# Spreading the output weights' eleven sums and moving later copies and the query weights' DMAs to ScalarE's queue, in one decoder layer

## Chip, cores and metric

The kernel runs on one core of one Trainium2 chip. The metric is the device time of one execution in microseconds (us). TensorE (PE) multiplies matrices, VectorE (DVE) and ScalarE (ACT) work element by element, GpSimd (POOL) does masks and issues the DMAs that add, SyncE (SP) issues nearly all other DMAs.

## The reference, cut to what matters

One layer of a decoder trunk in fp32: 512 positions of width 1024, and 256 memory tokens.

```python
h = rms_norm(x, norm_mix)
q, k, v, u, gate_b, gate_c, g_a, g_b = split(h @ w_in)
o_a = stick_breaking_attention(q, k, v)              # 8 heads x 64, causal
y_b = gate_b * causal_depthwise_conv(gate_c * u, conv_w)
merged = sigmoid(g_a) * (o_a @ w_branch_a) + sigmoid(g_b) * (y_b @ w_branch_b)
x = x + merged @ w_mix_out
x = x + memory_cross_attention(rms_norm(x), rms_norm(mem), w_mem_q, w_mem_kv, w_mem_o)
gate, up = split(rms_norm(x) @ w_ffn_in)              # hidden width 2816
x = x + (silu(gate) * up) @ w_ffn_out
return rms_norm(x, norm_final)
```

## The kernel before

Every fp32 product is made of three matmuls on parts: a tile is split into a high part (ACT's cast, line 156 and its like) and a low part (DVE's subtraction, line 157), and `mm3` multiplies high by high, high by low and low by high. A weight tile of 512 KB is loaded by SP (`load_w`, line 148, tile `wr`), cast by ACT (`wh`) and subtracted by DVE (`wl`); each of the three has a ring of four buffers.

Three of the products use a scheme of seven products of half-size blocks instead of eight (query projection of the memory attention, both FFN products). Its weight forms are sums of weight blocks, made on the way:

- **Output weights.** `w_ffn_out` comes as eleven tiles of four quarters each (`wfo_d[j]`). For each of them a DRAM tile `sums[j]` is formed by DMAs alone. `out_sums(j)` returns four steps: two plain copies from DRAM to DRAM (768 KB and 256 KB, line 569, issued on SP), then an adding DMA of two quarters of the weights (512 KB, line 572, issued on POOL), and twice an adding DMA of one quarter of the sums onto another (256 KB, line 572). Each step waits for the transfers of the step before it. The sums are read back only in the last product, from 709.9 us on.
- **Query weights.** `w_mem_q` comes as four tiles (heads) of 1 MB. For each head `form_load` loads the tile into SBUF (tile `pq`, two buffers, line 642), `form_sums` makes four additions on DVE (line 648) and `form_store` writes the tile to DRAM (`qsums`, line 652). `pair_forms` reads it back in the memory attention (line 810).

The order around the change is written by hand. A counter `started` advances by one at each call of `tick`. `job(at, steps, lag)` puts the steps of one sum on ticks `at`, `at + lag`, and so on; `tick` issues what stands on its number. Ticks 0 to 16 stand in the loop over the sixteen steps of the stick-breaking attention (four pairs of heads by four key blocks) and its end, 17 to 24 in the branch loop over eight output tiles, 25 to 28 in the mix-out product at every second tile, 29 and 30 in the memory keys' loop, 31 after the first half of the memory values, 32 to 35 in the four heads of the memory attention. `SUMS_AT` holds the tick of the first step of each of the eleven sums; the first `SPARSE` of them have a lag of 2 ticks, the others of 1. `after(i, last)` orders an instruction behind another in the schedule without a wait on the chip: a DMA that waits for no data is issued as soon as its queue comes to it.

In the attention stage SP also carries the query and key moves (line 361): for each pair of heads, parts of a tile are copied between the two halves of the partitions, six moves for the queries and three for the keys, some of which wait for earlier ones to land. POOL carries the causal masks (line 417) and, in tick 9's iteration, the store of the memory factors `rmd` (line 557).

In the memory keys' loop the row of squares' means goes to DRAM and back (`turned_row`, lines 226 and 228, on SP), since it has to be turned from a row to a column.

The branch loop's calls on the query weights:

```python
loaded_at, stored_at = {0: 0, 2: 1, 4: 2, 5: 3}, {3: 0, 5: 1, 7: 2}
summed_at = {2: 0, 4: 1, 6: 2, 7: 3}
```

The last store comes after the mix-out product's second tile.

Of the kernel before, what the change touches and what calls it, by code (L numbers as in the profile page):

```python
# [34 lines left out]
FIRST = 4  # L35
LIGHT = 3
BEHIND = 6
SUMS_AT = (0, 2, 4, 20, 22, 24, 25, 26, 27, 28, 30)
SPARSE = 3

O_Q, O_K, O_V, O_U, O_GB, O_GC, O_A, O_B = 0, 512, 1024, 1536, 2048, 2560, 3072, 4096

# [2 lines left out]
def hybrid_layer(ctx: ExitStack, tc: tile.TileContext, xT_d, memT_d, mem_d, cols_d, wv_d, win_d,  # L45
                 wbr_d, wmix_d, wmq_d, wmk_d, wmv_d, wmo_d, wfi_d, wfo_d, gfin_d, out):
    nc = tc.nc
# [16 lines left out]
    def nm(s):  # L64
        count[0] += 1
        return f"{s}{count[0]}"
# [4 lines left out]
    def tmp(s, cols=512):  # L71
        return tpool.tile([P, cols], F32, tag="t", name=nm(s), padded_shape=[P, 512])
# [34 lines left out]
    def after(i, earlier):  # L107
        for e in earlier:
            tc.add_manual_dep(i.ins, e.ins.name, mybir.DependencyInfo(
                mybir.DependencyClass.NoSync, mybir.DependencyReason.DATA), reason="order")  # L110
# [33 lines left out]
    def load_w(src, cols=P):  # L144

        k = D // cols
        raw = wpool.tile([P, D], F32, tag="wr", name=nm("wr"))
        i = nc.sync.dma_start(raw, src)
        loads.append(i)
        if count[1] < FIRST:  # L150
            count[1] += 1
            chained(i)
        hi = wpool.tile([P, k, cols], F32R, tag="wh", name=nm("wh"))
        lo = wpool.tile([P, k, cols], F32R, tag="wl", name=nm("wl"))
        h2, l2 = (t.rearrange("p k c -> p (k c)") for t in (hi, lo))
        after(nc.scalar.copy(h2, raw), lead[-1:])  # L156
        lows.append(nc.vector.tensor_tensor(out=l2, in0=raw, in1=f(h2), op=ALU.subtract))  # L157
        return hi, lo
# [292 lines left out]
    def scores(p, kt):  # L451
        c0, n = span(kt)
        keys = slice(kt * P, (kt + 1) * P)
        zs[p, kt] = []
        for hs in heads_of(kt):
            bank = ztile("z")
            zs[p, kt].append(bank)
            for i, h in enumerate(hs):
                for part in range(2):
                    nc.tensor.matmul(bank[:, i * n:(i + 1) * n], ks[p][h][:, keys],  # L460
                                     qs[p][h][part][:, c0:], start=i + part == 0, stop=part == 1,
                                     skip_group_check=True)
        for hs, bank in zip(heads_of(kt), zs[p, kt]):
            w = len(hs) * n
            z = bank[:, :w]
            e = tmp("e")[:, :w]
            nc.scalar.activation(e, z, AF.Abs)
            nc.scalar.activation(e, e, AF.Exp, scale=-1.0)
            nc.scalar.activation(e, e, AF.Ln, bias=1.0)
            nc.vector.scalar_tensor_tensor(out=e, in0=z, scalar=0.0, in1=e, op0=ALU.max,  # L470
                                           op1=ALU.add)
            causal(by_head(e, n))
            urgent.append(lambda *last, e=e, hs=hs: fails(p, kt, hs, e, n, last))
# [86 lines left out]
    def quarters(w):  # L560
        return w.rearrange("p (s c) -> p s c", s=4)

    def in_dram(tag):
        return dpool.tile([P, 4, 512], F32, tag=tag, name=nm(tag))

    sums = [in_dram(f"sums{j}") for j in range(NJ)]

    def copied(to, of):
        return lambda *last: after(nc.sync.dma_start(to, of), last)

    def added(to, of):
        return lambda *last: after(nc.gpsimd.dma_start(to, of, accum_op=ALU.add), last)  # L572

    def out_sums(j):
        t, w = sums[j], quarters(wfo_d[j])
        return ([copied(t[:, 1:4, :], w[:, 1:4, :]), copied(t[:, 0:1, :], w[:, 3:4, :])],
                [added(t[:, 0:4:3, :], w[:, 0:2, :])], [added(t[:, 1:2, :], t[:, 0:1, :])],
                [added(t[:, 2:3, :], t[:, 1:2, :])])

# [2 lines left out]
    def job(at, steps, lag=1):  # L582
        for n, some in enumerate(steps):
            jobs.setdefault(at + n * lag, []).extend(some)
# [19 lines left out]
    settle_behind()  # L604
    qsums = [in_dram(f"qsums{h}") for h in range(MH)]
    for j, n in enumerate(SUMS_AT):
        job(n, out_sums(j), 2 if j < SPARSE else 1)

    for i in range(len(steps) + 1):
        tick(*exps[-1:])  # L610
# [10 lines left out]
        if i + 1 < len(steps):  # L621
            to = lambda: scores(*steps[i + 1])
# [15 lines left out]
    mg, mgs, qraws = [], [], {}  # L638

    def form_load(h, last):  # L640
        qraws[h] = prepool.tile([P, 4, 512], F32, tag="pq", name=nm("pq"))
        after(nc.sync.dma_start(qraws[h], quarters(wmq_d[h])), last)

    def form_sums(h, last, *steps):

# [3 lines left out]
                                          op=ALU.add), last)  # L649

    def form_store(h):
        nc.sync.dma_start(qsums[h], qraws.pop(h))

    def mem_split(k2, last):
        mk = xpool.tile([P, 2, MEM], F32, tag="x", name=nm("mk"))
# [15 lines left out]
    for m in range(KD):  # L671
        sig = []
        for j in range(2):
            if (m, j) not in gates:
                gate(m, j)
            t = gates.pop((m, j))
            sigmoid = nc.scalar.activation(t, t, AF.Sigmoid)
            after(sigmoid, exps[-2:])
            sig.append(t)
        if m in summed_at:  # L680
            form_sums(summed_at[m], [sigmoid], (0, 0, 3), (3, 1, 3))
        w = load_w(wbr_d[m])
        for j in (1, 0):
            if m == 0 and j == 0:
                gate(EARLY, 0)
            ps = mmtile("br")
            gemm(ps, w, (oT, yb)[j], 4 * j)
            nc.vector.tensor_tensor(out=sig[j], in0=ps, in1=sig[j], op=ALU.mult)
        nc.vector.tensor_tensor(out=sig[0], in0=sig[0], in1=sig[1], op=ALU.add)
        merged.append(split(sig[0], "m"))  # L690
        if m in stored_at:
            form_store(stored_at[m])
        if m in loaded_at:
            form_load(loaded_at[m], [sigmoid])
        if m in summed_at:
            form_sums(summed_at[m], [sigmoid], (1, 1, 0), (2, 2, 1))
        tick(sigmoid)
        sigmoids.append([sigmoid])
        if m < KD // 2:
            mem_split(m, [sigmoid])  # L700
# [56 lines left out]
    def residual(w_dram, act, old, gain, formed):  # L757
# [4 lines left out]
        for m in range(KD):  # L762
            w = load_w(w_dram[m])
            ps = mmtile("r")
            gemm(ps, w, act)
            if old is None:
                xm = xpool.tile([P, S], F32, tag="x", name=nm("x"))
                after(nc.sync.dma_start(xm, xT_d[m * P:(m + 1) * P, :]), sigmoids[m // 2 - 4])
            else:
                xm = old[m]  # L770
            nc.vector.tensor_tensor(out=xm, in0=ps, in1=xm, op=ALU.add)
            xs.append(xm)
            if old is None and m % 2:
                tick(lows[-1])
                if qraws:
                    form_store(MH - 1)
            raw = f(unit("xr"))
            nc.scalar.activation(raw, xm, AF.Copy, scale=gain[:, m:m + 1])
            if m % 2:
                xf.append(formed(even, raw))  # L780
            else:
                even = raw
            if m == 0:
                nc.scalar.activation(acc, xm, AF.Square)
            else:
                sq = tmp("sq")
                nc.scalar.activation(sq, xm, AF.Square)
                nc.vector.tensor_tensor(out=acc, in0=acc, in1=sq, op=ALU.add)
# [87 lines left out]
    for m in range(KD):  # L876
        w = load_w(wmk_d[m])
# [8 lines left out]
        t = tmp("km", MEM)  # L886
# [52 lines left out]
    for h in range(MH):  # L939
        q = qgot[h]  # L940
        scs = []
        for t2 in range(2):
            ps = ztile("sc")
            scs.append(ps)
            for i in range(2):
                t = 2 * t2 + i
# [5 lines left out]
        for t2 in range(2):  # L952
# [14 lines left out]
            for i in range(2):  # L967
                t = 2 * t2 + i
# [25 lines left out]
        for j in range(2):  # L994
# [3 lines left out]
            for m in range(MT):  # L998
                w = vm[m][c // 512]
# [245 lines left out]
    def one_cast(j):  # L1245
        if j % 2 == 0:
            n = min(2, NJ - j)
            raw = ows["q3"] = wpool.tile([P, 2, 512], F32, tag="wr", name=nm("wr"))
            nc.sync.dma_start(raw[:, :n, :], wfo_d[j:j + n, :, 0:512].rearrange("j p c -> p j c"))
        raw = ows["q3"][:, j % 2, :]  # L1250
        pool, tag = (fpool, "wg") if j in (BEHIND, BEHIND + 2) else (wpool, ("wh", "wl")[j % 2])
        w = pool.tile([P, 2, 512], F32R, tag=tag, name=nm("wq"))
        nc.scalar.copy(w[:, 0, :], raw)
        ows[5, j] = w[:, 0, :], w[:, 1, :]
        return raw, *ows[5, j]
# [75 lines left out]
    n = uses.index((NF - 2, 5))  # L1331
# [23 lines left out]
    with tc.manual_schedule(engines={mybir.EngineType.PE, mybir.EngineType.Activation,  # L1355
# [58 lines left out]
        for j in range(2, NJ - 2):  # L1414
# [6 lines left out]
            if NJ - 2 - LIGHT <= j + 1 < NJ - 2 + 1:  # L1421
                n = j + 1 - (NJ - 2 - LIGHT)
                if n < LIGHT:
                    t34_of(n, halves(acts[n][1])[0])
        last = NJ - 2, NJ - 1
# [93 lines left out]
        w = one_cast(NJ - 1)  # L1519
# [184 lines left out]
```

## Time and profile before

| | |
|---|---|
| median of 3 runs | 835.94 us (835.62 to 836.13) |
| profiled execution | 837.15 us, span 835.4 us |
| mean granted TensorE clock | 0.998 |
| TensorE busy | 826.5 us, 99% of the span, 4518 matmuls |
| VectorE busy | 689.6 us, 83% |
| ScalarE busy | 481.8 us, 58% |
| GpSimd busy | 105.9 us, 13% |
| DMA on SP's and ACT's own queues | 130.96 MB and 0.28 MB |
| DMA on POOL's queue | 23.21 MB |
| first copy to last copy of the sums on SP | 27.8 to 373.7 us |
| query weights: first load to last store on SP | 186.7 to 300.4 us |

Idle time is put down to the instruction that ended it. "SPq" and "ACTq" are the queues' own instructions: a DMA's duration there is the time of its issue, and its landing is given apart. A transfer's issue holds the instructions behind it on the same engine.

### The profile page before, as it was taken

Reading aid. Unit: us, or ns where it says so; the run is one execution under the profiler, and the core shown is the slowest. Engines: PE = TensorE matmul, PEld = TensorE weight load, DVE = VectorE, ACT = ScalarE, POOL = GpSimd, SP = SyncE. Lnnn points to the kernel's source line nnn. Section 1 sums busy time; section 2 is a strip of 40 time slices with the busy share of each in tenths; the row PEclk is TensorE's granted clock in tenths of the full one; section 3 lists DMA queues with packets and bytes.
Section 4 is the critical chain, followed back from the end, with each engine's and each line's share of the span. In section 5 each row is a group of like instructions: output and inputs, shape, how many; then the busy total and the mean of one; then the engine's idle time right before and its main releaser. Section 6 shows DMA issues by size and latency. Waiting matters only on the chain.

```text
span 835.4 us, 12382 instructions
## 1 busy us (share of the span) xinstructions
PE 826.5 (99%) x4518; PEld 718.7 (86%) x4518; DVE 689.6 (83%) x1146; ACT 481.8 (58%) x836; POOL 105.9 (13%) x131
## 2 busy tenths in 40 slices
PE   9999999999999999999999999999999999999996
PEld 7888888888888888888999789999999999888885
DVE  7879899995665557865677689999999999999886
ACT  7567777674332345645665556645555555576664
POOL 0022331120010011210000131111111110000301
PEclk9999999999999999999999999999999999999999
DMA  8667965224588999898445626677777773565552
GB/s 303 202 189 179 222 141 121 82 81 171 216 225 291 253 312 294 194 218 279 125 136 189 167 50 170 165 179 189 207 179 196 181 181 97 166 217 198 178 187 100
DMA packets 58926, 155.24 MB, mean 186 GB/s; under 512 B 6545, under 2 KB 7825, under 8 KB 57842
## 3 DMA queue, kind: packets, MB, share of 16 engines
q1 hardware_dynamic: 46226, 130.96, 46.6%
q0 software_dynamic: 12352, 23.21, 18.5%
q8 instruction: 35, 0.57, 0.3%
q10 hardware_dynamic: 288, 0.28, 0.1%
q14 instruction: 25, 0.20, 0.1%
HBM read 144.08 MB, written 29.37 MB: 208 GB/s over the span
## 4 chain that ended last, share of the span: by engine, by line
PE 95%; DMA 2%; DVE 1%; ACT 1%; issue 0%; DVEq 0%; SPq 0%; ACTq 0%
PE z L1078 13%; PE p L1389 12%; PE pr L161 8%; PE pr L162 8%; PE pr L163 8%; PE y L1073 5%; PE r L161 3%; PE r L163 3%; PE r L162 3%; PE v L288 3%; PE y L1081 2%; PE v L1073 2%; PE qz L834 2%; PE br L162 2%; PE br L161 2%; PE br L163 2%
## 5 line engine op out<-in xcount | busy, mean ns | idle before, releaser
L156 ACT CAST wh<-wr 128x1024 fp32r<-128x1024 f32 x76 | 79.7, 1051 | 113.0 <-issue 45.1
L161 PE MATMUL pr<-xgh,wh 128*128 128x512 f32 x288 | 112.7, 391 | 0.0
L162 PE MATMUL pr<-xgl,wh 128*128 128x512 f32 x288 | 112.4, 390 | 0.0
L163 PE MATMUL pr<-xgh,wl 128*128 128x512 f32 x288 | 112.3, 390 | 0.0
L157 DVE TENSOR_TENSOR wl<-wr,wh 128x1024 fp32r<-128x1024 f32 x76 | 93.6, 1232 | 9.8 <-ACT wh L156 9.5
L163 PEld LDWEIGHTS pr<-xgh,wl 128*128 128x128 f32 x288 | 54.1, 188 | 11.5
L161 PEld LDWEIGHTS pr<-xgh,wh 128*128 128x128 f32 x288 | 54.1, 188 | 10.6
L162 PEld LDWEIGHTS pr<-xgl,wh 128*128 128x128 f32 x288 | 54.1, 188 | 10.5
L1026 POOL DMA_DIRECT2D ws<-in_w_ffn_in_dram x22 | 26.6, 1207 | 237.5 <-PE pt L987 57.1
L1078 PE MATMUL z<-xd,wf 128*128 128x256 f32 x360 | 47.5, 282 | 0.0
L1110 ACT COPY sa<-z 128x256 f32<-128x256 f32 x44 | 16.5, 374 | 52.1 <-PE z L1078 52.0
L1078 PEld LDWEIGHTS z<-xd,wf 128*128 128x128 f32 x360 | 44.9, 190 | 0.1
L1170 DVE TENSOR_TENSOR wf<-wg,wf 128x1024 fp32r<-128x1024 f32 (+1 forms) x44 | 43.1, 979 | 1.5
L1170 DVE TENSOR_TENSOR wl<-wr,wh 128x1024 fp32r<-128x1024 f32 x33 | 41.1, 1247 | 3.6 <-ACT wh L1237 3.6
L368 DVE TENSOR_TENSOR g<-pr,r0b 128x512 f32<-128x512 f32 x16 | 11.0, 689 | 34.2 <-PE pr L163 34.2
L1237 ACT CAST wh<-wr 128x1024 fp32r<-128x1024 f32 x33 | 34.5, 1049 | 6.9 <-PE xt L1474 2.5
L1078 PE MATMUL z<-xf,wf 128*128 128x256 f32 x264 | 35.4, 283 | 0.0
L1078 PE MATMUL z<-xc,wf 128*128 128x256 f32 x264 | 35.1, 282 | 0.0
L1078 PEld LDWEIGHTS z<-xf,wf 128*128 128x128 f32 x264 | 33.4, 192 | 0.1
L1078 PEld LDWEIGHTS z<-xc,wf 128*128 128x128 f32 x264 | 33.0, 190 | 0.0
L572 POOL DMA_DIRECT2D sums<-sums x22 | 18.5, 851 | 94.7 <-DMA sums<-in_w_ffn_out_dram 47.4
L572 POOL DMA_DIRECT2D sums<-in_w_ffn_out_dram x11 | 15.7, 1469 | 98.7 <-DMA sums<-in_w_ffn_out_dram 98.2
(377 smaller groups left out, 2313.8 us busy)
## 6 DMA issues: line engine op xcount, KB each, us to landing
wr<-in_w_in_dram SPq DMA_DIRECT2D x36, 512.0 KB, 4.1
ws<-in_w_ffn_in_dram SPq DMA_DIRECT2D x22, 512.0 KB, 4.6
wg<-in_w_ffn_in_dram SPq DMA_DIRECT2D x22, 512.0 KB, 4.5
ws<-in_w_ffn_in_dram POOLq DMA_DIRECT2D x22, 512.0 KB, 5.8
wr<-sums SPq DMA_DIRECT2D x22, 512.0 KB, 4.4
sums<-in_w_ffn_out_dram SPq DMA_DIRECT2D x11, 768.0 KB, 8.1
wr<-in_w_ffn_out_dram SPq DMA_DIRECT2D x16, 512.0 KB, 4.5
sums<-in_w_ffn_out_dram POOLq DMA_DIRECT2D x11, 512.0 KB, 10.2
```

The costliest lines, as they stand in the source:

```text
L156: after(nc.scalar.copy(h2, raw), lead[-1:])
L157: lows.append(nc.vector.tensor_tensor(out=l2, in0=raw, in1=f(h2), op=ALU.subtract))
L161: nc.tensor.matmul(ps, a[0], b[0], start=start, stop=False, **kw)
L162: nc.tensor.matmul(ps, a[0], b[1], start=False, stop=False, **kw)
L163: nc.tensor.matmul(ps, a[1], b[0], start=False, stop=stop, **kw)
L572: return lambda *last: after(nc.gpsimd.dma_start(to, of, accum_op=ALU.add), last)
L1026: nc.gpsimd.dma_start(s13, a[:, 0:4:3, :], accum_op=ALU.add)
L1073: nc.tensor.matmul(ps, hi, both[0], start=i < 3 and k == 0, stop=False, skip_group_check=True)
L1078: nc.tensor.matmul(ps[:, :HS], a, b, start=i < 3 and k == 0 and j == 0, stop=k == KP - 1 and j == 2, skip_group_check=True)
L1170: nc.vector.tensor_tensor(out=lo, in0=src, in1=f(hi), op=ALU.subtract)
L1237: nc.scalar.copy(hi, raw)
L1389: nc.tensor.matmul(res[i][s2], a[:, ts], b, start=j == 0 and n == 0, stop=n == 2 and j == (BEHIND - 1 if (i, s2) == (5, 1) else NJ - 1))
```

## The change

`SUMS_AT` becomes wider: sum 0 stays at tick 0; sums 1, 2 and 3 start at ticks 3, 6 and 9 (2, 4 and 20 before); sums 4, 5 and 6 at 20, 22 and 24 (22, 24 and 25 before); sums 7 to 10 at 26, 28, 30 and 32 (26, 27, 28 and 30 before). The first four sums, not three, have a lag of 2. The copies of sums 4 to 10 are issued by ACT instead of SP; those of sums 0 to 3 stay on SP. The query weights' four loads and four stores are issued by ACT instead of SP. All adding DMAs stay on POOL. No arithmetic, tile or transfer is added or left out.

```diff
-SUMS_AT = (0, 2, 4, 20, 22, 24, 25, 26, 27, 28, 30)
-SPARSE = 3
+SUMS_AT = (0, 3, 6, 9, 20, 22, 24, 26, 28, 30, 32)
+SPARSE = 4
...
-    def copied(to, of):
-        return lambda *last: after(nc.sync.dma_start(to, of), last)
+    def copied(queue, to, of):
+        return lambda *last: after(queue.dma_start(to, of), last)
...
-    def out_sums(j):
+    def out_sums(j, queue):
         t, w = sums[j], quarters(wfo_d[j])
-        return ([copied(t[:, 1:4, :], w[:, 1:4, :]), copied(t[:, 0:1, :], w[:, 3:4, :])],
+        return ([copied(queue, t[:, 1:4, :], w[:, 1:4, :]),
+                 copied(queue, t[:, 0:1, :], w[:, 3:4, :])],
                 [added(t[:, 0:4:3, :], w[:, 0:2, :])], [added(t[:, 1:2, :], t[:, 0:1, :])],
                 [added(t[:, 2:3, :], t[:, 1:2, :])])
...
-        job(n, out_sums(j), 2 if j < SPARSE else 1)
+        job(n, out_sums(j, nc.sync if j < SPARSE else nc.scalar), 2 if j < SPARSE else 1)
...
-        after(nc.sync.dma_start(qraws[h], quarters(wmq_d[h])), last)
+        after(nc.scalar.dma_start(qraws[h], quarters(wmq_d[h])), last)
...
-        nc.sync.dma_start(qsums[h], qraws.pop(h))
+        nc.scalar.dma_start(qsums[h], qraws.pop(h))
```

## The prediction

> **What bounds the kernel now.** I read the page first (busy time, chain that ended last), then TensorE's own waits, then TensorE in order of time at those waits, then what the late inputs waited for.
>
> ```profile
> span 835.4 us, 12382 instructions
> PE 826.5 (99%) x4518; PEld 718.7 (86%) x4518; DVE 689.6 (83%) x1146; ACT 481.8 (58%) x836; POOL 105.9 (13%) x131
> ...
> PE 95%; DMA 2%; DVE 1%; ACT 1%; issue 0%; DVEq 0%; SPq 0%; ACTq 0%
> ```
>
> TensorE (PE) is busy for 826.5 of 835.4 us and holds 95% of the chain. The change takes no matmul away and adds none, so it can gain only where PE waits. These are all the waits that the profile shows for it:
>
> ```profile
> PE warm L248 <- DVE neg L92: 1.4, 1, 1.4
> PE qz L834 <- ACT qs L845: 0.7, 1, 0.7
> PE vm L161 <- DVE km L888: 0.4, 1, 0.4
> ```
>
> The first is before the first tick. The other two, in order of time (columns: start, duration):
>
> ```profile
> 366.96 0.39 PE L161 MATMUL vm<-wh,mg 128*128 128x512 f32 x1
> 367.37 0.50 PE L162 MATMUL vm<-wl,mg 128*128 128x512 f32 x1
> 367.71 0.40 PE L163 MATMUL vm<-wh,mg 128*128 128x512 f32 x1
> 368.52 0.50 PE L161 MATMUL vm<-wh,mg 128*128 128x512 f32 x1 [0.42 <-DVE km L888]
> 368.85 0.39 PE L162 MATMUL vm<-wl,mg 128*128 128x512 f32 x1
> ...
> 384.59 0.28 PE L834 MATMUL qv<-xfh,wf 128*128 128x256 f32 x1
> 385.58 0.39 PE L834 MATMUL qz<-xfh,wf 128*128 128x256 f32 x1 [0.71 <-ACT qs L845]
> ```
>
> A 512-column matmul starts 0.33 us after another even here (368.52 to 368.85). Against that pace, 366.96 to 368.52 holds three starts and 1.56 us, so 0.6 us is lost (up to 0.9 us if the undisturbed pace is shorter); at 384.59 the next start is 0.99 us off, of which a 256-column matmul takes at most 0.28, so 0.7 to 0.9 us is lost. **The most that the change can win is therefore about 1.8 us, 0.22% of 835.94.** Both losses lie behind late transfers:
>
> ```profile
> 354.73 5.07 DMA row<-vrow
> 359.81 5.61 DMA vr<-row
> ```
>
> ```profile
> 365.45 0.30 ACT L125 ACTIVATE ry<-vr,eps_t 128x4 f32<-128x4 f32 x1 [4.30 <-DMA vr<-row]
> 384.21 1.05 ACT L156 CAST wh<-wr 128x1024 fp32r<-128x1024 f32 x1 [1.11 <-DVE qa L843]
> ```
>
> The chain that ended last goes through a 2 KB row stored and loaded again in 10.7 us; ScalarE (ACT) stands 4.30 us for it and the casts behind it come late. At 384 ACT stands 1.11 us at a weight cast, and the read of a bank (L845) that PE needs is behind it.
>
> **The change part by part.**
>
> *Query weights' loads and stores, eight DMAs of 1 MB, from SyncE (SP) to ACT; and the two copies of jobs 4 to 10, fourteen DMAs.* Their issue costs on SP, and the one issue late on ACT's queue:
>
> ```profile
> L569 SPq DMA_DIRECT2D sums<-in_w_ffn_out_dram x22: 496/588/1357, 27.8 to 373.7; - x22
> L642 SPq DMA_DIRECT2D pq<-in_w_mem_q_dram x4: 378/428/1117, 186.7 to 259.9; - x4
> L652 SPq DMA_DIRECT2D qsums<-pq x4: 326/328/332, 218.8 to 300.4; - x4
> 831.93 0.35 ACTq L1589 DMA_DIRECT2D out_dram<-l  x1
> ```
>
> ACT gains 14 x 0.588 + 4 x 0.428 + 4 x 0.328 = 11.3 us of issue (bounds: 22 x 0.35 = 7.7 us by ACT's own row, 14 x 1.357 + 4 x 1.117 + 4 x 0.332 = 24.8 us by the longest). It also takes over the wait of a store for VectorE's (DVE's) sums:
>
> ```profile
> SPq L652 <- DVE pq L648: 8.5, 4, 2.1
> ACT wh L156 <- PE pr L162: 33.0, 13, 4.8
> ```
>
> That is 2.1 us a store, and the weight casts (L156) and sigmoids are queued behind it. What covers this in the branch and mix-out stages, from 187 to about 340 us: ACT itself waits for PE to give back a buffer of `wh` (33.0 us in 13 waits), so casts run a ring of four ahead, and ACT is busy for little of the time there:
>
> ```profile
> 240.00:260.00 20.00, 20.00 (x90) 16.58 (x89) 11.87 (x15) 6.42 (x8) 1.67 (x2) 1.00 0.88 272
> 260.00:280.00 20.00, 20.00 (x90) 16.57 (x89) 7.94 (x10) 5.30 (x7) 2.00 (x2) 1.00 0.87 269
> 360.00:380.00 20.00, 19.57 (x101) 16.28 (x100) 12.00 (x23) 9.96 (x18) 1.62 (x2) 1.00 0.90 238
> ```
>
> (Columns: stretch, its length, busy time and count of PE, PEld, DVE, ACT, POOL, then clock, DMA share, GB/s.) A store and a load together hold ACT for at most 2.1 + 0.33 + 1.12 = 3.6 us against 13 us idle in 20. I take 0; uncovered, four such stands would be 14 us, which I leave out of the range, since the next casts are a ring ahead. SP loses 22 issues and 8.5 us of waits; PE shows no wait in that stretch, so this gains 0 as well.
>
> *Jobs 9 and 10, whose copies now go out at ticks 30 and 32.* Job 9's two copies come on ACT where job 10's came on SP (373 us), job 10's in the first head, about 400 us. Two issues are 2 x 0.588 = 1.2 us each time (0.7 to 2.7), in a stretch where ACT, DVE and PE hang on each other closely. At tick 30 ACT has 10 us idle in 20, but two PE losses show that little of it is cover. Bounds: -0.1 (SP's 1.14 us of issue is gone from before a query load) to +2.7 each; I take +0.3 for both together, near the covered end, because PE shows no wait at all after 386 us.
>
> *Fewer sums at a time from tick 24 to 31.* Of the ticks 24 to 28 five started a job before, three do now. An add is slow and the row's trip lay among them:
>
> ```profile
> sums<-in_w_ffn_out_dram SPq DMA_DIRECT2D x11, 768.0 KB, 8.1
> sums<-in_w_ffn_out_dram POOLq DMA_DIRECT2D x11, 512.0 KB, 10.2
> r<-row POOLq DMA_DIRECT2D x1, 2.0 KB, 3.2
> ```
>
> The same kind of 2 KB load took 3.2 us elsewhere, against 5.61. By the ticks, jobs 8 and 9 both stood between first and last add at the row's trip (tick 29); now it is job 8 and the end of job 7. If each half of the trip falls by 1 to 2 us, ACT's stand of 4.30 us shrinks to between 0.3 and 2.3 us, and the first loss (0.6 to 0.9) goes in part or whole. I take half, -0.4, from 0 to -0.9. The second loss keeps its cause, since job 9's copies now stand where job 10's did: 0, from -0.9 to +0.9 (as much again if the same cast is late by its 1.11 us twice).
>
> *Job 3 from tick 20 to tick 9, jobs 1 and 2 one and two ticks later.* In the attention stage SP issues eight copies rather than six, and POOL twelve adds, not nine, among the causal masks. One place is tight: the last pair of heads, whose query and key moves stand on SP.
>
> ```profile
> 117.92 15.18 SPq L361 DMA_DIRECT2D qk<-qk  x6
> 133.84 7.19 SPq L361 DMA_DIRECT2D qk<-qk  x3
> ```
>
> ```profile
> L361 SPq DMA_DIRECT2D qk<-qk x1: 462/462/462, 140.6 to 140.6; - x1
> DMA to landing us min/median/max: 2.2/2.2/2.2
> ```
>
> ```profile
> L460 PE MATMUL z<-qk,qk x4: 220/274/276, 145.2 to 145.5; 128*128 128x128 f32 x4
> ```
>
> ```profile
> L557 POOL DMA_DIRECT2D rmd<-rm x1: 788/788/788, 120.6 to 120.6; - x1
> DMA to landing us min/median/max: 12.1/12.1/12.1
> ```
>
> The last key move lands at 140.6 + 2.2 = 142.8, PE needs it at 145.2: cover 2.4 us. Tick 9 is the one whose memory factors POOL stores at 120.6, so job 3's copies come on SP near 120, among the six query moves, and move 1 MB beside a store that takes 12.1 us. A pair of copies lands 8.1 us after issue. Bounds: the moves are late by 0 (the copies run in the 15.18 us in which SP mostly stands) to 8.1 us, so PE loses 0 to 8.1 - 2.4 = 5.7. I take 0 as the likelier, because SP's chain of six moves is mostly standing, with 5.7 kept as the end. POOL's wait before an add can hold a mask too; it shares that price.
>
> **Sum.** 0 + 0 + 0.3 - 0.4 + 0 + 0 = -0.1 us. The profiled execution took 837.15 (span 835.4 and 1.75 around it), 0.14% over the median of 835.94, so it would take 837.05, and the median 835.8.
>
> **The rivals.** *Slower through the last pair of heads* (other side): job 3's copies hold up the chain of moves. For it: 2.4 us of cover, nine moves one after another, transfers of 12.1 us just there. Against it: earlier pairs of heads had copies beside their moves without a PE wait. With a pair of copies in full ahead, 8.1 - 2.4 = 5.7 us, 841.6; at the middle of the price, 4.1 - 2.4 = 1.7, up to 837.6; I put its typical time at 839, 3 us of loss. It decides from 4.1 us of lateness (2.4 of cover and 1.7 of bound). [...]
>
> ```profile
> L572 POOL DMA_DIRECT2D sums<-sums x1: 873/873/873, 124.8 to 124.8; - x1
> DMA to landing us min/median/max: 12.2/12.2/12.2
> ```
>
> ```profile
> L361 SPq DMA_DIRECT2D qk<-qk x1: 462/462/462, 125.6 to 125.6; - x1
> DMA to landing us min/median/max: 12.0/12.0/12.0
> ```
>
> They landed at 137.0 and 137.6, one behind the other.
>
> *Slower through ACT in the cross-attention*: job 9 or 10's issues, or a longer string of adds from 380 to 440, hold a cast or an exponential. For it: the 1.11 us stand was enough for a loss; against it: no PE wait after 386. Both pairs uncovered give +2.4, 838.3; it decides from 1.7 us uncovered.
>
> *Faster*: both losses go, -1.8, 834.1. For it: less traffic at the row's trip; against it: job 9's copies at 373. [...]
>
> *The queues make no difference*: SP's relief and ACT's load are both hidden and the two losses stay: 835.9, inside no change.
>
> **How the numbers follow.** About 0.2% (1.7 us) is what a measurement can tell from no change. Forecast and the rival without effect, within 0.2%: 0.57. Last pair of heads beyond 1.7 us: 0.22. ACT beyond 1.7 us: 0.12. Faster by both losses: 0.09. So faster 0.09, same 0.57, slower 0.34. Time 835.8. Range 834.2 to 839.5: below it only the full gain, above it the part of the first rival beyond 3.6 us, together under 0.2.
>
> **What would show it.** In the changed kernel: L642, L652 and most of L569 on ACT's queue; no PE wait between 187 and 340; the row's store and load shorter than 5.07 and 5.61; the L845 wait still there; the last key move landing before PE's L460 of the fourth pair. The prediction is wrong if PE waits for L460 or L506 (masks or moves late) or for a cast whose ACT idle time ends with a query store, or if waits before 825 us fall by more than 1.8.

## The result, and the profile after

| | before | changed |
|---|---|---|
| median | 836.04 us (835.62 to 836.39, one run more than above) | 846.61 us (846.26 to 847.65, 4 runs) |
| profiled execution | 837.15 us, span 835.4 | 846.77 us, span 845.1 |
| mean granted TensorE clock | 0.998 | 0.995 |

The changed kernel is slower: ratio 1.0129, 95% interval 1.0111 to 1.0146, 10.6 us between the medians and 9.7 us between the two spans. The forecast of 835.8 and its range up to 839.5 were wrong. (What the prediction calls "jobs" are the sums; lines of `kernel.py` after the new function head are one higher than before.)

The page of the changed kernel, its head and the shares of the chain that ended last:

```profile
span 845.1 us, 12387 instructions
PE 828.5 (98%) x4518; PEld 719.8 (85%) x4518; DVE 690.7 (82%) x1146; ACT 480.9 (57%) x836; POOL 104.3 (12%) x131
...
PE 92%; DMA 3%; DVE 2%; issue 1%; ACT 1%; ACTq 0%; DVEq 0%; SPq 0%
```

PE has only 2.0 us more busy time but holds 92% of the chain, not 95%: time went into waiting. All its waits (total, times, longest, in us; "issue" means that the profile shows no releaser):

```profile
PE z L460 <- issue: 6.8, 1, 6.8
PE warm L248 <- DVE neg L92: 1.4, 1, 1.4
PE qz L835 <- ACT qs L842: 1.3, 1, 1.3
PE z L506 <- DVE l L432: 0.6, 1, 0.6
```

Two are new, L460 and L506; the wait at L161 is gone; the one at the query projection (L834 before, L835 now) is 1.3 where it was 0.7. The large one in order of time on PE (start, duration):

```profile
145.18 0.39 PE L162 MATMUL pr<-xgl,wh 128*128 128x512 f32 x1
145.40 0.39 PE L163 MATMUL pr<-xgh,wl 128*128 128x512 f32 x1
...
153.31 1.09 PE L460 MATMUL z<-qk,qk 128*128 128x128 f32 x4 [6.84 <-issue]
...
155.16 0.63 PE L163 MATMUL pr<-xgh,wl 128*128 128x512 f32 x1
155.59 0.63 PE L161 MATMUL pr<-xgh,wh 128*128 128x512 f32 x1
...
156.84 0.40 PE L161 MATMUL pr<-xgh,wh 128*128 128x512 f32 x1
```

L460 is the fourth pair of heads. It started at 145.21 before and starts at 153.31 now. And the wait costs more than its own length. Matmuls that started 0.22 us apart ahead of it (145.18, 145.40) start 0.43 us apart behind it (155.16, 155.59) and last 0.63 instead of 0.39 us, until 156.84. The same stretches by the granted clock (the column before the last two), of the changed kernel:

```profile
145.00:150.00 5.00, 1.47 (x7) 0.89 (x5) 4.57 (x8) 0.76 (x2) 1.75 (x3) 1.00 0.55 85
150.00:155.00 5.00, 1.69 (x6) 1.62 (x7) 0.68 (x2) 0.53 (x2) 0.00 (x0) 0.50 1.05 321
155.00:160.00 5.00, 5.00 (x20) 4.09 (x20) 2.43 (x4) 2.89 (x6) 1.40 (x3) 0.82 0.47 121
```

The clock was 0.50, then 0.82; before, it was 1.00 in each of these stretches. The half pace lasts from 153.31 to 156.84, 3.5 us.

From the starts of the same matmul in both traces (changed minus before), the way to +9.7 us is: +1.1 right behind the L506 near 114 us (114.80 before, 115.90 now) and up to L460, +8.1 at L460, +9.8 once the clock is back (147.03 before, 156.84 now), +9.0 behind the old wait at L161 (368.52, 377.51), +10.3 at the query projection (381.74, 392.08), +9.5 behind the old wait there (385.58, 395.05), +9.7 at the end. So L460 has 7.0 us, the slow clock behind it 1.7, L506 1.1, and the rest nearly cancels.

Why L460's moves were late: SP's queue in the changed kernel (start, time of issue; six query moves, then three key moves, L361), and POOL's DMAs of that time:

```profile
120.96 5.95 SPq L361 DMA_DIRECT2D qk<-qk  x5
126.96 7.22 SPq L569 DMA_DIRECT2D sums<-in_w_ffn_out_dram  x1
134.29 0.54 SPq L361 DMA_DIRECT2D qk<-qk  x1
134.88 0.93 SPq L569 DMA_DIRECT2D sums<-in_w_ffn_out_dram  x1
...
136.94 10.80 SPq L361 DMA_DIRECT2D qk<-qk  x3
```

```profile
122.90 0.78 POOL L557 DMA_DIRECT2D rmd<-rm  x1 [4.27 <-DVE rm L133]
...
124.10 0.89 POOL L572 DMA_DIRECT2D sums<-sums  x1
...
125.64 0.85 POOL L572 DMA_DIRECT2D sums<-sums  x1 [0.16 <-issue]
...
146.02 1.19 POOL L572 DMA_DIRECT2D sums<-in_w_ffn_out_dram  x1 [1.06 <-ACT l L431]
```

And what one line's DMAs took to land, in the same trace: the second of these adds, and the last key move, which releases PE:

```profile
L572 POOL DMA_DIRECT2D sums<-sums x1: 847/847/847, 125.6 to 125.6; - x1
DMA to landing us min/median/max: 15.6/15.6/15.6
```

```profile
L361 SPq DMA_DIRECT2D qk<-qk x1: 461/461/461, 147.3 to 147.3; - x1
DMA to landing us min/median/max: 5.9/5.9/5.9
```

Before, one add stood behind the factors' store `rmd`; now there are two, at 124.10 and 125.64, and the store goes out at 122.90 instead of 120.62. Between the fifth and the sixth query move stands the first copy of sum 3, whose *issue* takes 7.22 us (0.588 was the median issue before). That made the moves little later. The sixth query move overwrites what the fourth reads, so it can go out only once the fourth has landed, here at 133.2 (issued at 122.8, 10.4 us to land). It went out at 134.29, so the copy's issue held it by about 1 us; in e7 below, with no copy there, it goes out at 134.2. What grows is the time to land: the copies take 17.4 and 10.6 us, and the second key move behind them 9.9 us instead of 6.5. The last key move overwrites what the first reads and waits for it. It is issued at 147.28 instead of 140.57, takes 5.9 us instead of 2.2, and lands at 153.2; PE goes on at 153.31. At 146.02, 1.3 us ahead of it, POOL issued sum 3's first add (512 KB).

### The profile page after: what moved, and what is told of

It reads as the page before. It is cut to its first block, busy times and chain, and to the rows that moved or that the text cites. A ratio compares the mean times of both kernels' runs of the same rounds, so it can differ in the third digit from the quotient of the medians.

```text
span 845.1 us, 12387 instructions
## 1 busy us (share of the span) xinstructions
PE 828.5 (98%) x4518; PEld 719.8 (85%) x4518; DVE 690.7 (82%) x1146; ACT 480.9 (57%) x836; POOL 104.3 (12%) x131
## 4 chain that ended last, share of the span: by engine, by line
PE 92%; DMA 3%; DVE 2%; issue 1%; ACT 1%; ACTq 0%; DVEq 0%; SPq 0%
PE z L1079 13%; PE p L1390 12%; PE pr L161 7%; PE pr L162 7%; PE pr L163 7%; PE y L1074 5%; PE r L163 3%; PE r L162 3%; PE r L161 3%; PE v L288 3%; PE qz L835 3%; PE y L1082 2%; PE v L1074 2%; PE qv L835 2%; PE br L163 2%; PE br L162 2%
## 5 line engine op out<-in xcount | busy, mean ns | idle before, releaser
L161 PE MATMUL pr<-xgh,wh 128*128 128x512 f32 x288 | 113.3, 393 | 0.0
L157 DVE TENSOR_TENSOR wl<-wr,wh 128x1024 fp32r<-128x1024 f32 x76 | 93.5, 1230 | 13.2 <-ACT wh L156 13.1
L161 PEld LDWEIGHTS pr<-xgh,wh 128*128 128x128 f32 x288 | 54.5, 189 | 10.8
L572 POOL DMA_DIRECT2D sums<-in_w_ffn_out_dram x11 | 13.7, 1243 | 110.0 <-DMA sums<-in_w_ffn_out_dram 108.6
```

What stands on the lines that cost most here:

```text
L161: nc.tensor.matmul(ps, a[0], b[0], start=start, stop=False, **kw)
```

## Experiments

Each diff is against the kernel before or the changed kernel, as named, and is cut to the lines that matter. Times are medians against runs of the kernel before on the same chip.

**The two halves of the change.** The new ticks alone, all DMAs on SP:

```diff
# before, with
+SUMS_AT = (0, 3, 6, 9, 20, 22, 24, 26, 28, 30, 32)
+SPARSE = 4
```

> The changed ticks and SPARSE = 4, every copy and all query DMAs still on SyncE. T1 (job 3's copies stand among the query and key moves of the last pair of heads on SP) and T2 (the adds of jobs 1 and 2 pile up behind the memory factors' store there): slower by 9 to 11 us against before, about 846, with TensorE's wait of some 7 us at L460 as in the changed kernel. T3 (what costs is ScalarE's queue): within 1.5 us of before, no wait at L460.

844.68 us, ratio 1.0108 (1.0092 to 1.0124). PE's waits:

```profile
PE z L460 <- issue: 7.5, 1, 7.5
...
PE z L506 <- DVE l L432: 0.6, 1, 0.6
```

The ticks alone give both new waits and some five sixths of the loss (8.8 of 10.6 us). Here the first copy's issue took only 3.96 us, and yet SP stood until the fourth query move had landed, at 135.1:

```profile
126.69 3.96 SPq L569 DMA_DIRECT2D sums<-in_w_ffn_out_dram  x1
135.14 0.46 SPq L361 DMA_DIRECT2D qk<-qk  x1
```

The queues alone:

```diff
# changed kernel, with
+SUMS_AT = (0, 2, 4, 20, 22, 24, 25, 26, 27, 28, 30)
+SPARSE = 3
```

> The ticks of before, with the copies from sum 3 on and the query weights' loads and stores on ScalarE's queue. T1 and T2: within 1.5 us of before (835 to 837.5), no wait at L460. T3: slower by 7 us or more, 843 or above.

838.95 us, ratio 1.0038 (1.0023 to 1.0052), and one wait is 2.3 us where it was 0.7:

```profile
PE qz L835 <- ACT qs L842: 2.3, 1, 2.3
```

Here the copies of sums 3 to 10 are on ACT. So at the old ticks the queues cost about 3 us on their own, more than the first two theories allowed and less than the third.

**Which ticks make the wait at L460.** Sum 3 early, all else as before; and the reverse, the changed kernel with sum 3 late, which keeps sums 1 and 2 at ticks 3 and 6:

```diff
# e3: before, with
+SUMS_AT = (0, 2, 4, 9, 22, 24, 25, 26, 27, 28, 30)
+SPARSE = 4
# e4: changed kernel, with
+SUMS_AT = (0, 3, 6, 18, 20, 22, 24, 26, 28, 30, 32)
+SPARSE = 3
```

> Before, with nothing changed but sum 3's first tick (20 to 9) and its lag (2). Sums 1 and 2 keep ticks 2 and 4. T1: the wait at L460 is there, 3 to 8 us, time 839 to 846. T2: only one add stands behind the factors' store as before, so no wait at L460 above 1 us, time 835 to 837. T3: no change.

> The changed kernel, with sum 3 taken out of the attention stage (first tick 18, lag 1, its copies on ScalarE); sums 1 and 2 stay at ticks 3 and 6. T1: no wait at L460 above 1 us, 835 to 837.5. T2: two adds still stand behind the factors' store, the key moves land some 4 us later, the cover of 2.4 us is used up and L460 waits 1.5 us or more: 838 to 841. T3: slower as the changed kernel.

836.56 us, ratio 1.0006 (0.9996 to 1.0015), and 836.70 us, ratio 1.0011 (1.0002 to 1.0021). Neither has the wait at L460. In the first, the copies stand at the same place on SP, with one add behind the store:

```profile
117.67 7.49 SPq L361 DMA_DIRECT2D qk<-qk  x5
125.20 0.59 SPq L569 DMA_DIRECT2D sums<-in_w_ffn_out_dram  x1
125.89 0.54 SPq L361 DMA_DIRECT2D qk<-qk  x1
126.48 5.51 SPq L569 DMA_DIRECT2D sums<-in_w_ffn_out_dram  x1
...
132.86 8.37 SPq L361 DMA_DIRECT2D qk<-qk  x3
```

The issue of the key moves ends at 141.2 (132.86 + 8.37), against 147.7 in the changed kernel and 141.0 before. In the second, two adds stand behind the store and no copies:

```profile
120.27 11.54 SPq L361 DMA_DIRECT2D qk<-qk  x6
...
132.54 10.21 SPq L361 DMA_DIRECT2D qk<-qk  x3
```

It ends at 142.8. Each alone takes 0.2 and 1.7 us of the 2.4 us of cover, and PE doesn't wait. A theory with one cause, sum 3's copies or the later ticks of sums 1 and 2, fell: the wait needs both.

**Where sum 3's copies stand.** In the changed kernel, sum 3 two ticks later; and sum 3's copies on ACT as well:

```diff
# e7: changed kernel, with
+SUMS_AT = (0, 3, 6, 11, 20, 22, 24, 26, 28, 30, 32)
# e6: changed kernel, with
+        job(n, out_sums(j, nc.sync if j < SPARSE - 1 else nc.scalar), ...)
```

> The changed kernel, with sum 3 at ticks 11, 13, 15, 17 instead of 9, 11, 13, 15: its copies come on SP behind the last key move. T4 and T5: only two adds are left behind the factors' store, as with sum 3 at tick 18: no wait at L460 above 1 us, 836 to 839.5. If any copies in the attention stage beside sums 1 and 2 cost the same: 843 or above.

> The changed kernel, with sum 3's two copies on ScalarE's queue as well. If the place on SP's queue is what counts (the copies' issue held SP for 7.2 us between two query moves): L460 waits 1 us or less, 837 to 840, unless the issue holds ScalarE in turn. T4 and T5 (the transfers are served in one order whatever the queue): the key moves still land after 150, L460 waits 4 us or more, 843 to 849.

At tick 11 the copies go out at 145.79, behind the last key move: 836.68 us, ratio 1.0007 (0.9996 to 1.0017), no wait at L460. Two ticks take away nearly the whole loss. SP's queue there, with the sixth query move's issue ending at 134.67 and no copy ahead of it:

```profile
121.62 13.05 SPq L361 DMA_DIRECT2D qk<-qk  x6
```

With the copies on ACT at tick 9: 843.35 us, ratio 1.0080 (1.0052 to 1.0109), four runs from 838.75 to 845.01. The profile is of the quickest of them:

```profile
PE z L460 <- issue: 0.4, 1, 0.4
```

Off SP, the copies no longer hold the moves' issue, and yet three of four runs lost 5 to 9 us, two of them at a mean clock of 0.994 (0.999 in the profiled run). That speaks for the transfers, not SP's time of issue, as the main cost, as e1 and e7 do. In the profiled run the store, both adds and the copies are all there, and L460 loses only 0.4 us:

```profile
L361 SPq DMA_DIRECT2D qk<-qk x1: 461/461/461, 145.0 to 145.0; - x1
DMA to landing us min/median/max: 2.3/2.3/2.3
```

This last key move goes out 0.3 us behind sum 3's first add (144.73) and lands in 2.3 us; in the changed kernel, e1 and e5 (below) the add is 1.3 to 1.6 us ahead, and the move takes 5.9 to 6.0 us. So some 3.7 us of the wait seem to hang on that add. No edit tried it alone, and no profile is of one of the three slow runs, so this part stays an inference.

**The factors' store.** Two edits meant to take `rmd` out of the way. The first moves its ticks only:

```diff
# e5: changed kernel, with
+MEAN_AT = 12
+ROW_AT = 15
```

> The changed kernel, with the memory factors taken at step 12 instead of 9 and read back at 15 instead of 13: their 1 KB store in 4-byte pieces (landing 10 to 13 us after issue in every run so far) no longer stands between the query and key moves. T4 (the store holds up what is queued behind it, and only sums 1 to 3 together then exceed the cover of 2.4 us): the moves land some 8 us earlier, no wait at L460 above 1 us, 836 to 839.5, what is left being the queues' part. T5 (the traffic of two adds and 1 MB of copies alone is enough): wait at L460 of 4 us or more, 842 or above.

845.26 us, ratio 1.0107 (1.0091 to 1.0122): a miss. POOL still issued the store at 123.82, as its DMA goes out when its data is there (POOL stood 3.54 us for `rm` just ahead of it), and L460 still lost 6.8 us, so it decides nothing. The second also orders the store behind a late exponential:

```diff
# e11: e5, with
-        nc.gpsimd.dma_start(d.rearrange("o (t p) -> p (o t)", p=P), rm)
+        after(nc.gpsimd.dma_start(d.rearrange("o (t p) -> p (o t)", p=P), rm), exps[-2:-1])
```

> The changed kernel, with the memory factors' store ordered behind step 10's exponential, so that it goes out after tick 12's add instead of at tick 9 (the earlier try left it where it was). T4 (the store in 4-byte pieces holds what is behind it): fourth query move landing within 8 us instead of 10 to 13, last key move landed before 146, no wait at L460 above 1 us, 836 to 839.5. T5 (traffic alone is enough): L460 waits 4 us or more, 842 or above.

836.16 us, ratio 1.0000 (0.9991 to 1.0008). The store now goes out at 153.54, and the SP queue with the same copies at the same place is:

```profile
120.86 5.95 SPq L361 DMA_DIRECT2D qk<-qk  x5
126.86 0.59 SPq L569 DMA_DIRECT2D sums<-in_w_ffn_out_dram  x1
127.55 0.64 SPq L361 DMA_DIRECT2D qk<-qk  x1
128.24 1.08 SPq L569 DMA_DIRECT2D sums<-in_w_ffn_out_dram  x1
...
130.16 10.51 SPq L361 DMA_DIRECT2D qk<-qk  x3
```

The landing of the second add, and of the last key move:

```profile
L572 POOL DMA_DIRECT2D sums<-sums x1: 846/846/846, 126.2 to 126.2; - x1
DMA to landing us min/median/max: 6.3/6.3/6.3
```

```profile
L361 SPq DMA_DIRECT2D qk<-qk x1: 461/461/461, 140.2 to 140.2; - x1
DMA to landing us min/median/max: 2.2/2.2/2.2
```

With the ticks, copies and adds of the changed kernel, the add lands in 6.3 us instead of 15.6, the fourth query move in 4.4 us instead of 10.4, the copy is issued in 0.59 us instead of 7.22, and there is no wait at L460. So the loss comes where three things meet before the last moves: a store of 1 KB that takes 11.2 us to land, the adds of sums 1 and 2 at their later ticks, two of them behind it, and 1 MB of copies. That each is needed is shown (e3 has the old ticks of sums 1 and 2, e4 and e7 no copies there, e11 no store). That the second add is what these ticks bring is not: in e3 the moves and the store also start 2 to 3 us earlier (117.67 and 120.63, against 120.96 and 122.90). The adds land at 139.1 and 141.2, behind the store's 134.1, and without the store at 128.6 and 132.5. By what mechanism the store makes them late isn't shown.

**What on ACT costs 3 us.** At the old ticks, only the copies of sums 3 to 10 on ACT; and only the query weights' DMAs:

```diff
# e8: before, with
+        job(n, out_sums(j, nc.sync if j < SPARSE else nc.scalar), ...)
# e9: before, with
+        after(nc.scalar.dma_start(qraws[h], quarters(wmq_d[h])), last)
+        nc.scalar.dma_start(qsums[h], qraws.pop(h))
```

> Before, with only the copies of sums 3 to 10 on ScalarE; ticks and query DMAs as before. T6 (on ScalarE the last sum's copies are no longer held behind a query load that waits for its buffer, so they go out some 2 us earlier, ahead of that load, and its landing makes ScalarE late): slower by 1 to 3 us, 837 to 839, with TensorE's wait at L835 of 1.5 us or more. T7 (the query weights' loads and stores are what costs on ScalarE): within 0.8 us of before.

> Before, with only the query weights' four loads and four stores on ScalarE. T6: within 0.8 us of before, 835.2 to 836.8. T7: slower by 1 to 3 us, 837 to 839.

838.68 us, ratio 1.0029 (1.0016 to 1.0043), and 835.86 us, ratio 0.9997 (0.9987 to 1.0008). The query weights' eight DMAs cost nothing that shows, the copies about 2.6 us. The copies' runs spread from 836.3 to 840.9, and the profile is of the quickest, so it can't say where. Split by sums:

```diff
# e13: e8, copies of sums 3 to 9 on ACT, sum 10 on SP
# e14: e8, copies of sum 10 alone on ACT
```

> The kernel before with the copies of sums 3 to 9 issued by ScalarE; those of sum 10 stay on SyncE, and so do the query weights' DMAs. If the last sum's copies are what costs (they leave 2.4 us earlier on ScalarE, ahead of the load of a query form), this is within 0.5 us of before, about 836.0, with a spread of runs like that of before. If any copies on ScalarE cost, for instance those of sums 3 to 9 beside the loads of the branch and mix-out stages, it stays near 838.7 and some runs pass 840.

> The kernel before with the copies of sum 10 alone issued by ScalarE. If the last sum's copies are what costs, about 838.5, with a wait of 0.4 to 2.3 us at the read of a bank in the query projection (line 835). If it is the others, about 836.0 with the wait as before, 0.7 us.

837.75 us, ratio 1.0026 (1.0012 to 1.0040), and 836.25 us, ratio 1.0003 (0.9995 to 1.0012): 2.1 and 0.6 us by the medians, about the 2.6 together, though the 0.6 alone is within the noise. My guess that the last sum's copies were the cause fell. PE's waits that differ from before, with sums 3 to 9 on ACT, then with sum 10 alone:

```profile
PE vm L162 <- DVE wl L157: 1.4, 1, 1.4
```

```profile
PE qz L835 <- ACT qs L842: 1.5, 1, 1.5
```

The first is at 368.98 us, where the low part of a weight tile comes late behind the row's trip. The row goes out at 354.98 and its load at 361.24, against 354.73 and 359.81 before, in a stretch where the DMA share rose:

```profile
350.00:360.00 10.00, 10.00 (x58) 8.68 (x57) 9.69 (x18) 5.20 (x11) 2.57 (x3) 1.00 1.00 175
```

1.00 here, 0.87 before, at no more bytes (175 and 178 GB/s). That wait is about what this execution's span is longer by than the profile before (836.6 against 835.4). Five of the 12 runs were above 839.5 us, four of these at a mean clock of 0.995 or 0.996, so they probably hold a longer wait somewhere; no profile fell on one. Nor is it shown that ACT's queue as such costs: these copies also go out 1.8 to 3.9 us later than on SP (the first at 231.12 instead of 227.24), and no run separates the two.

At the new ticks, little of this cost is left: e4 and e11, with the late ticks and ACT's issues of the change, took 836.70 and 836.16 us, and e12 below, with the same late ticks and everything on SP, 836.28.

**The wait at L506.** All copies on SP and the late sums spread; the attention stage's ticks varied, sum 3 late:

```diff
# before, SPARSE 3, with SUMS_AT = (..., 18, 20, 22, 24, 26, 28, 30, 32) and ahead of it
# e10: 0, 2, 4     e12: 0, 3, 6     e15: 0, 3, 4     e16: 0, 2, 6
```

> Before, with ticks (0, 2, 4, 18, 20, 22, 24, 26, 28, 30, 32), SPARSE = 3 and everything on SyncE: the attention stage as before, the later sums two ticks apart. If fewer sums in flight at the row's trip shorten it and copies on SP behind the query loads do no harm: the losses at 367 and 385 of 0.6 to 0.9 us each fall, 834.2 to 835.9. Otherwise 836 to 837.

> Sum 3 at tick 18 and lag 1, sums 1 and 2 at ticks 3 and 6, late sums as in the changed kernel, everything on SyncE. If sums 1 and 2 at ticks 3 and 6 cost the wait of 0.6 us at L506 seen in the changed kernel and the queues cost the rest: 835.3 to 836.2, between the all-SyncE version with ticks 2 and 4 (834.93) and the one with queues (836.7), L506 waiting 0.6.

> All copies on SyncE, the late sums spread as in the candidate, sum 1 at tick 3 and sum 2 at tick 4. If sum 1's adds are what comes into the low parts' way, the wait of 0.6 us at line 506 is there and the time is about 836.2; if not, no such wait, and 834.9 as for ticks 2 and 4.

> All copies on SyncE, the late sums spread as in the candidate, sum 1 at tick 2 and sum 2 at tick 6. If sum 2's steps are what comes in the way, the wait of 0.6 us at line 506 is there and the time is about 836.2; if it is sum 1, no such wait and 834.9; if it takes both, neither this kernel nor that with sum 1 later shows the wait.

| sums 1 and 2 at | median, us | ratio | wait at L506 |
|---|---|---|---|
| 2, 4 | 834.93 | 0.9987 (0.9978 to 0.9996) | none |
| 3, 6 | 836.28 | 0.9997 (0.9989 to 1.0006) | 0.6 |
| 3, 4 | 835.99 | 1.0003 (0.9994 to 1.0011) | 0.6 |
| 2, 6 | 835.13 | 0.9988 (0.9979 to 0.9996) | none |

Sum 1 at tick 3 makes the wait; sum 2's tick doesn't matter. The first and the last row beat both kernels. All waits of PE in the first:

```profile
PE warm L248 <- DVE neg L92: 1.4, 1, 1.4
```

Both old losses, at 367 and 385 us, are gone, with all DMAs on SP: the spread of the late sums over more ticks (with sum 3 at tick 18, which neither kernel has) is the part of the change that pays, 1.1 us (0.13%) by the medians.

## Why the prediction was wrong

- **"Job 3 from tick 20 to tick 9, jobs 1 and 2 one and two ticks later", taken as 0 with 5.7 us as its end: this step failed.** It measured 7.0 us at L460. The place, the 2.4 us of cover and the store of 12.1 us were all in the prediction; the rival *Slower through the last pair of heads* named the late moves and gave them 0.22. The reason given for 0 was that SP's chain of moves is "mostly standing" in its 15.18 us. But SP stood because the transfers ahead hadn't landed. Copies put into that stand cost little with the old ticks of sums 1 and 2 (e3, 0.2 us of the cover), and much with the later ones behind the store. The end was too low, too: the last key move landed 10.4 us later than before (153.2, 142.8), where the prediction allowed 8.1. It priced the copies at their median landing of 8.1 us, and here they took 17.4 and 10.6; it had no term for a second add behind the store, nor for sum 3's own first add just ahead of the last move, and that move took 3.7 us longer to land. Of the 10.4 us, the cover took 2.4 and the 1.1 by which PE itself came later; the rest is the wait.
- **A wait's cost was taken as its length.** The rival had no term for the clock: 1.7 us more behind the wait.
- **Masks late (L506), named as a sign of error**, cost 1.1 us, by sum 1's tick (e15, e16). What came late was a low part on DVE (L432), not a mask of POOL; why DVE reached it later was not shown.
- **Copies on ACT, +0.3 for two late ones and 0 for the rest:** +2.6 in all at the old ticks. Sum 10 measured 0.6 (bounds up to 2.7 held it), but sums 3 to 9, taken as covered, 2.1; by which path isn't shown. At the new ticks, which are the change's own, the changed kernel less e1 gives about 1.8 by the medians (10.6 less 8.8) with overlapping intervals, but without the wait at L460 next to nothing is left (e4, e11, e12). So this term isn't shown to be wrong for the change itself.
- **Query weights' DMAs, 0:** right (e9), and no PE wait between 187 and 340 us came up.
- **First loss, −0.4 by a shorter trip of the row:** the direction was right, and it went whole (0.8 us, from +9.8 to +9.0). In the changed kernel:

```profile
364.58 2.12 DMA row<-vrow
366.75 7.49 DMA vr<-row
```

  The store fell from 5.07 to 2.12, but the load rose from 5.61 to 7.49; 1.07 us together, not 1 to 2 each.
- **Second loss, 0:** a wait stayed there, at another bank (L842), 1.3 for 0.7. The profiles of e4, e5, e6, e7 and e11, with the same late ticks and ACT's issues, have none there, so these ticks and issues do not by themselves make it.

## What to carry to other kernels

SP stood in a chain of small DMAs because it waited for transfers (25.2 us in seven waits in the profile before), so its idle time was not by itself room for larger ones: add up what is in flight ahead of the last move of such a chain, all queues together, before counting any cover. A long issue in the trace need not be what costs (of 7.22 us about 1 us counted here): ask what the next instruction would have waited for without it. Price the additions of a change that meet at one place together, not one by one, and add the slow clock to a long wait of TensorE (1.7 us behind 6.8 here). Ordering one tiny slow store away, or moving a copy by two ticks, was worth more than any choice of queue.

## What was not expected of the hardware

- A store of 1 KB, 256 numbers from 128 partitions, took 9.4 to 13.1 us to land (e11, e7; 12.1 before, 11.2 in the changed kernel). The adds issued behind it on POOL's queue took 12.2 us before, 15.0 and 15.6 in the changed kernel, 10.3 in e3, 13.2 and 14.2 in e4. The fifth query move, issued behind it on SP's queue, landed after it in these profiles: at 137.6 against 132.7 before, 141.4 against 134.1 in the changed kernel. With the store out of the way, the two adds took 4.7 and 6.3 us (e11).
- The issue of one copy on SP took 7.22, 3.96 and 6.31 us (changed kernel, e1, e5) with these transfers pending, and 0.59 us without the store (e11).
- The same copies issued by ACT instead of SP, at the old ticks, cost 2.6 us and widened the spread of runs (836.3 to 840.9, against 834.6 to 838.0). The wait that the slowest of these runs hold stays open, as it does for sum 3's copies on ACT at tick 9.
